# Regrouping the first columns of an input projection, and pinning the first solve on VectorE, in a FoX and RWKV-7 layer

## The chip, the cores and the metric

The kernel runs on one core of a Trainium2 chip. The metric is the device time of one execution in microseconds (us), and the time before is the median of three runs. PE is TensorE, the matrix engine; DVE is VectorE; ACT is ScalarE; POOL is GpSimd; SP is SyncE, which here does nothing but issue DMA transfers. Each engine works through its own list of instructions in the order in which they were placed at compile time and waits where an operand or a buffer is not ready.

## The reference

One layer over 256 tokens of width 4096, in float32. One input projection feeds two groups of heads and a gate; the two are joined, gated, projected, and added to the residual with a LayerNorm:

```
proj = einsum('bsd,dc->bsc', x, w_in)      # q,k,v,f | r,k,v,w_down,a_down | z
fox  = attention(q, k, v, cumsum(log_sigmoid(f + f_bias)))          # 16 heads of 128
r,k,v,w,a = token_shift(rw columns, mu_shift)
decay = exp(-exp(-softplus(-(w0 + tanh(w) @ w_up)) - 0.5));  a = sigmoid(a0 + a @ a_up)
y = rwkv7_scan(r, decay, k, v, -kk, kk * a)                         # 32 heads of 64
h = concat(fox, groupnorm(y) + bonus) * silu(z)
x = layernorm(ALPHA * x + h @ w_out)
```

The low-rank parts `w_down` and `a_down` have 96 columns each, and the forget gate `f` has 16: together the 208 columns that the kernel calls LoRA columns.

## The kernel before, in words

**The projections.** A float32 operand is split into a rounded high part and the remainder (`split`, L136 to L142): ACT casts the high part (L140), DVE subtracts (L141). A product of two such operands takes three matmuls (`mm`, L144 to L148): high by high (L146), low by high (L147), high by low (L148). The stationary operand is a 128 by 128 piece of the transposed tokens, the moving one a row of weights, up to 512 columns wide. The contraction runs over 32 slices of 128 (`KT`).

**The opening (L109 to L171).** It computes the 208 LoRA columns and the first block of 512 projection columns together, since the tokens are loaded and split at the same time. The slices come in 17 pieces, two of one slice and fifteen of two. Each piece brings tokens (`xr`), LoRA weights (`lr`) and main weights (`wr`). For each piece PE does the LoRA matmuls (into `accl`, two PSUM tiles for the two halves of the tokens) and then the 512-column ones (into `acc0_0`).

**The pairs.** After that the work goes by 8 pairs `n` of RWKV heads (each pair also with two FoX heads), each with four blocks `b` of 512 columns, each of 16 weight chunks of two slices; `w_3_7` is chunk 7 of block 3 of the current pair, and the profile leaves the numbers of pair and block out and writes `w_7`. A chunk is 12 matmuls. Chunks are prefetched: raw weights in 4 buffers (`wr`), high parts in 4, low parts in 3. While PE multiplies, generators are advanced by one step every six matmuls (`slot()`): they turn `bk` (the block's result, copied from PSUM) through DRAM, prepare the chunk matrices, run FoX attention and the RWKV recurrence.

**The solve (`rwkv`, L573 to L586).** For each pair the inverse of triangular 32 by 32 blocks is formed by 31 back-substitution steps on DVE. Each step is a product (L579, into `prod`) and a sum (L582, into `xc`), and each is one step of the generator. The result goes to DRAM (`td`) and back (`T`), is transposed into `X` (L610), and PE uses `T` and `X` in `qt` (L616) and `xp` (L637).

**What sets the order.** The compiler's list scheduler orders each engine's instructions by priorities and modelled times. `tc.keep_in_program_order(...)` pins one instruction to its place in the program among those of its engine. In the solve only the first product of each pair (`if not t`) is pinned. DMA transfers issued by SP form one queue in a fixed order: one that waits holds all behind it.

**The forget gate.** `lora()` transposes the LoRA result on PE (`lwt` L309, `fft` L312), and `forget()` turns it into a cumulative sum that goes to DRAM as `ncd` (L351), by way of `flg` (L350). `lw`, the copy of the LoRA result, shares one buffer with `bk` (tag `bk`), so the first `bk` is filled only when the transposes have read `lw`.

Of the kernel before, what the change touches and what calls it, by code (L numbers as in the profile page):

```python
# [10 lines left out]
F32 = mybir.dt.float32  # L11
# [6 lines left out]
P = 128  # L18
S = 256
D = 4096  # L20
KT = D // P
# [12 lines left out]
OB = 512  # L34
# [24 lines left out]
C_ROW = C_SCAN + S  # L59
C_W = C_ROW + 2  # L60
LW = 2 * LORA + NF


def constants():
# [17 lines left out]


@with_exitstack
def layer(ctx: ExitStack, tc: tile.TileContext, xt, xtok, w_lora, w_main, muv, w_o, up, par, mulora, fbias, lng, lnb, cst, out):
    nc = tc.nc
    PS = bass.MemoryType.PSUM

# [24 lines left out]
    for n, (k0, k1) in enumerate(pieces):  # L113
        raw = spool.tile([P, 2 * S], F32, tag="xr", name=f"xr{n}", bufs=4)
        nc.sync.dma_start(out=raw[:, : (k1 - k0) * S], in_=xt[:, k0:k1, :].rearrange("p k t -> p (k t)"))
        x_raw.append(raw)
        raw = spool.tile([P, 2 * LW], F32, tag="lr", name=f"lr{n}", bufs=4)
        (nc.scalar if n < 3 else nc.sync).dma_start(out=raw[:, : (k1 - k0) * LW], in_=w_lora[:, k0:k1, :].rearrange("p k c -> p (k c)"))
        l_raw.append(raw)
        raw = wpool.tile([P, 1024], F32, tag="wr", name=f"wr{n}", bufs=4)  # L120
        nc.sync.dma_start(out=raw[:, : (k1 - k0) * OB], in_=w_main[0, 0][:, k0:k1, :].rearrange("p k c -> p (k c)"))
        w_raw.append(raw)
    warm = const.tile([1, 1], F32, name="warm")
    nc.vector.memset(warm, 0.0)
# [12 lines left out]
    def split(src, n, name, pool=wpool, tag="", cols=1024):  # L137
        hi = pool.tile([P, cols], F32R, tag="wh" + tag, name=name + "h", bufs=4 if pool is wpool else 1)
        lo = pool.tile([P, cols], F32R, tag="wl" + tag, name=name + "l")
        nc.scalar.copy(hi[:, :n], src[:, :n])  # L140
        nc.vector.tensor_tensor(lo[:, :n], src[:, :n], hi[:, :n].bitcast(F32), ALU.subtract)  # L141
        return hi, lo  # L142

    def mm(acc, at, k, hi, lo, o, n):  # L144
        tt = slice(at * P, (at + 1) * P)
        nc.tensor.matmul(acc[:, :n], xs[k][:, 0, tt], hi[:, o : o + n], start=(k == 0), stop=False)  # L146
        nc.tensor.matmul(acc[:, :n], xs[k][:, 1, tt], hi[:, o : o + n], start=False, stop=False)  # L147
        nc.tensor.matmul(acc[:, :n], xs[k][:, 0, tt], lo[:, o : o + n], start=False, stop=(k == KT - 1))  # L148
# [8 lines left out]
    for n, (k0, k1) in enumerate(pieces):  # L157
        for k in range(k0, k1):
            t = xpool.tile([P, 2, S], F32R, tag=f"x{k}", name=f"x{k}")
            r = x_raw[n][:, (k - k0) * S : (k - k0 + 1) * S]  # L160
            tc.keep_in_program_order(nc.scalar.copy(t[:, 0, :], r))
            nc.vector.tensor_tensor(t[:, 1, :], r, t[:, 0, :].bitcast(F32), ALU.subtract)
            xs.append(t)
        hi, lo = split(l_raw[n], (k1 - k0) * LW, f"wl{n}", spool, str(n % 3), 2 * LW)
        for j, m in steps(k1 - k0, False):
            mm(acc_l[m], m, k0 + j, hi, lo, j * LW, LW)
        hi, lo = split(w_raw[n], (k1 - k0) * OB, f"wr{n}")
        for j, m in steps(k1 - k0, k1 == KT):
            mm(acc_0[m], m, k0 + j, hi, lo, j * OB, OB)
    early.close()  # L170

    half = const.tile([P, 2, G], F32, name="half")
# [123 lines left out]
        return r  # L296

    lr = const.tile([LORA, 2, 2, S], F32R, name="lr")
    lw = rp.tile([P, 2, LW], F32, tag="bk", name="lw")
    for m in range(2):  # L300
        nc.scalar.copy(lw[:, m, :], acc_l[m][:, :LW])
    ff = []

    def lora():
# [200 lines left out]
    def rwkv(n):  # L505
# [71 lines left out]
        for t, s in enumerate(range(B - 2, -1, -1)):  # L577
            w = B - 1 - s
            first = nc.vector.tensor_tensor(prod[:, :, :, s + 1 :], nb[:, :, s : s + 1, s + 1 :].to_broadcast([P, 2, NJ, w]), xc[:, :, :, s + 1 :], ALU.mult)  # L579
            if not t:  # L580
                tc.keep_in_program_order(first)
            nc.vector.tensor_reduce(xc[:, :, :, s : s + 1], prod[:, :, :, s:], AX.X, ALU.add)  # L582
            next(other, None)
            if t % ROWS == ROWS - 1:
                yield
# [453 lines left out]
def arrange(inputs):  # L1039
# [9 lines left out]
    res["w_lora"] = np.ascontiguousarray(np.concatenate([wd, ad, ff], 1).reshape(KT, P, LW).transpose(1, 0, 2))  # L1049
# [35 lines left out]
```

## Time and profile before

| | |
|---|---|
| median of three runs | 1958.2 us (1957.36 to 1959.06) |
| profiled execution, span from first to last instruction | 1956.1 us |
| PE busy | 1937.4 us, 99% |
| DVE busy | 1368.3 us, 70% |
| ACT busy | 981.2 us, 50% |
| mean DMA rate | 215 GB/s |
| granted TensorE clock, mean | 0.998 |

The profile gives the span of the one profiled execution and no other time for it; the median of the runs is 2.1 us above that span, and this difference is kept as it is. PE is busy for almost the whole span, so time can be won only where PE waits, or where its matmuls take more time than their columns need. In the timelines a row has start, duration, engine, line, operation, output and inputs, form and count, and in square brackets the idle time before it with what ended it. Matmuls overlap: their pace is read from the distance between starts, not from their durations.

### The profile page before, as it was taken

The page shows a single profiled execution, that of the slowest core. Times are in us where ns is not written, and L with a number is a line of the kernel's source. Part 1 is how long each engine was busy: PE and PEld are TensorE (multiplying, and loading weights), DVE is VectorE, ACT ScalarE, POOL GpSimd, SP SyncE. Part 2 cuts the span into 40 slices and gives each one's busy share as a digit, 9 for nine tenths or more (in the row PEclk, how much of TensorE's full clock was granted, in tenths as well). Part 3 has the DMA queues.
Part 4 walks back from the last instruction along what each step waited for, and adds up shares of the span by engine and source line. Part 5 has one row for each costly group of instructions (what it writes and reads, how often), then busy time and mean ns, then how long its engine had stood idle before and what let it go on. Part 6 is the DMA issues. An engine that isn't in the chain of part 4 may idle for free.

```text
span 1956.1 us, 28202 instructions
## 1 busy us (share of the span) xinstructions
PE 1937.4 (99%) x10169; PEld 1586.9 (81%) x10169; DVE 1368.3 (70%) x2212; ACT 981.2 (50%) x1485; POOL 81.2 (4%) x111
## 2 busy tenths in 40 slices
PE   9998999999999999999999999999999999999998
PEld 7887778888887888788878887888788878888886
DVE  6587667866886688667857785778577856755555
ACT  6553555455545554565456545644564454433332
POOL 0010001000100010001000100010001000000000
PEclk9999999999999999999999999999999999999999
DMA  9577657867686778676867686778677777766564
GB/s 337 145 237 198 206 163 244 226 194 213 212 233 186 215 215 232 192 220 208 232 185 225 208 236 183 225 209 234 178 231 211 241 274 236 255 199 199 189 198 168
DMA packets 269392, 420.13 MB, mean 215 GB/s; under 512 B 142338, under 2 KB 171028, under 8 KB 269252
## 3 DMA queue, kind: packets, MB, share of 16 engines
q1 hardware_dynamic: 268820, 417.91, 70.7%
q8 instruction: 80, 1.31, 0.3%
q10 hardware_dynamic: 432, 0.43, 0.1%
q14 instruction: 60, 0.49, 0.1%
HBM read 388.61 MB, written 29.64 MB: 214 GB/s over the span
## 4 chain that ended last, share of the span: by engine, by line
PE 86%; DMA 1%; DVE 0%; ACT 0%; issue 0%; DVEq 0%; ACTq 0%; SPq 0%
PE acc L146 21%; PE acc L148 20%; PE acc L147 20%; PE oacc L852 6%; PE oacc L854 6%; PE oacc L853 6%; PE yp L678 1%; PE gp L517 1%; PE up L653 1%; PE rh L626 1%; PE sp L662 0%; DMA wo<-in_w_o_dram 0%; PE fsp L717 0%; PE fop L736 0%; PE tp L550 0%; DMA h<-hd 0%
## 5 line engine op out<-in xcount | busy, mean ns | idle before, releaser
L582 DVE TENSOR_REDUCE xc<-prod 128x8 f32<-128x16 f32 (+30 forms) x248 | 73.2, 295 | 6.7
L579 DVE TENSOR_TENSOR prod<-Nb,xc 128x8 f32<-128x8 f32 (+30 forms) x248 | 71.6, 289 | 6.6
L141 DVE TENSOR_TENSOR w_10l<-w,w_10h 128x1024 fp32r<-128x1024 f32 x31 | 37.9, 1223 | 37.8 <-PE acc L148 21.6
L141 DVE TENSOR_TENSOR w_6l<-w,w_6h 128x1024 fp32r<-128x1024 f32 x31 | 38.9, 1256 | 34.9 <-ACT w_6h L140 18.6
L141 DVE TENSOR_TENSOR w_8l<-w,w_8h 128x1024 fp32r<-128x1024 f32 x31 | 37.8, 1219 | 32.9 <-ACT UV L656 13.6
L141 DVE TENSOR_TENSOR w_0l<-w,w_0h 128x1024 fp32r<-128x1024 f32 x31 | 37.9, 1222 | 31.3 <-ACT w_0h L140 14.8
L141 DVE TENSOR_TENSOR w_5l<-w,w_5h 128x1024 fp32r<-128x1024 f32 x31 | 38.3, 1235 | 29.3 <-PE acc L148 17.4
L148 PE MATMUL acc<-w_7l,x 128*128 128x512 f32 x124 | 49.5, 399 | 5.4 <-DVE w_7l L141 5.4
L141 DVE TENSOR_TENSOR w_7l<-w,w_7h 128x1024 fp32r<-128x1024 f32 x31 | 37.9, 1222 | 22.3 <-PE acc L148 13.2
L141 DVE TENSOR_TENSOR w_11l<-w,w_11h 128x1024 fp32r<-128x1024 f32 x31 | 37.9, 1222 | 21.0 <-PE acc L148 13.5
L141 DVE TENSOR_TENSOR w_12l<-w,w_12h 128x1024 fp32r<-128x1024 f32 x31 | 37.5, 1211 | 20.6 <-PE acc L148 16.1
L141 DVE TENSOR_TENSOR w_14l<-w,w_14h 128x1024 fp32r<-128x1024 f32 x31 | 38.0, 1227 | 19.9 <-issue 11.1
L140 ACT CAST w_0h<-w 128x1024 fp32r<-128x1024 f32 x31 | 32.7, 1053 | 38.3 <-PE acc L147 21.7
L140 ACT CAST w_5h<-w 128x1024 fp32r<-128x1024 f32 x31 | 32.6, 1053 | 37.9 <-PE acc L147 37.9
L140 ACT CAST w_8h<-w 128x1024 fp32r<-128x1024 f32 x31 | 32.6, 1050 | 37.7 <-DMA w<-in_w_main_dram 31.3
L146 PE MATMUL acc<-w_7h,x 128*128 128x512 f32 x124 | 51.0, 411 | 0.0
L140 ACT CAST w_13h<-w 128x1024 fp32r<-128x1024 f32 x31 | 32.5, 1049 | 36.4 <-PE acc L147 22.9
L146 PE MATMUL acc<-w_5h,x 128*128 128x512 f32 x124 | 50.5, 408 | 0.0
L146 PE MATMUL acc<-w_8h,x 128*128 128x512 f32 x124 | 50.0, 404 | 0.4 <-ACT w_8h L140 0.4
L140 ACT CAST w_9h<-w 128x1024 fp32r<-128x1024 f32 x31 | 32.4, 1046 | 35.6 <-PE acc L147 32.9
L146 PE MATMUL acc<-w_3h,x 128*128 128x512 f32 x124 | 50.2, 405 | 0.0
L140 ACT CAST w_7h<-w 128x1024 fp32r<-128x1024 f32 x31 | 32.6, 1052 | 34.9 <-PE acc L147 19.7
(813 smaller groups left out, 6549.3 us busy)
## 6 DMA issues: line engine op xcount, KB each, us to landing
w<-in_w_main_dram SPq DMA_DIRECT2D x496, 512.0 KB, 3.9
wo<-in_w_o_dram SPq DMA_DIRECT2D x128, 512.0 KB, 3.8
bt<-bk SPq DMA_DIRECT2D x88, 128.0 KB, 4.0
Nb<-nd SPq DMA_DIRECT2D x16, 512.0 KB, 5.0
wr<-in_w_main_dram SPq DMA_DIRECT2D x15, 512.0 KB, 7.1
hd<-hl SPq DMA_DIRECT2D x29, 256.0 KB, 4.4
h<-hd SPq DMA_DIRECT2D x29, 256.0 KB, 6.1
raw<-bt SPq DMA_DIRECT2D x16, 256.0 KB
```

What stands on the lines that cost most here:

```text
L140: nc.scalar.copy(hi[:, :n], src[:, :n])
L141: nc.vector.tensor_tensor(lo[:, :n], src[:, :n], hi[:, :n].bitcast(F32), ALU.subtract)
L146: nc.tensor.matmul(acc[:, :n], xs[k][:, 0, tt], hi[:, o : o + n], start=(k == 0), stop=False)
L147: nc.tensor.matmul(acc[:, :n], xs[k][:, 1, tt], hi[:, o : o + n], start=False, stop=False)
L148: nc.tensor.matmul(acc[:, :n], xs[k][:, 0, tt], lo[:, o : o + n], start=False, stop=(k == KT - 1))
L517: nc.tensor.matmul(gp[u][j][:, c * P : (c + 1) * P], BK[h, u, c, :], lt[j][h, u, c, :], start=True, stop=True)
L579: first = nc.vector.tensor_tensor(prod[:, :, :, s + 1 :], nb[:, :, s : s + 1, s + 1 :].to_broadcast([P, 2, NJ, w]), xc[:, :, :, s + 1 :], ...
L582: nc.vector.tensor_reduce(xc[:, :, :, s : s + 1], prod[:, :, :, s:], AX.X, ALU.add)
L626: nc.tensor.matmul(rh[HALF[j], u * C : (u + 1) * C], lt[j][:, u, c, 0:C], SV[j][:, u, c, :], start=True, stop=True)
L852: nc.tensor.matmul(acc, ht[k][:, 0, tt], hi, start=(k == 0), stop=False)
L853: nc.tensor.matmul(acc, ht[k][:, 1, tt], hi, start=False, stop=False)
L854: nc.tensor.matmul(acc, ht[k][:, 0, tt], lo, start=False, stop=(k == KT - 1))
```

## The change

Two things change. First, in the opening the LoRA array gets 128 more columns: it holds the 208 LoRA columns and the first 128 of the first block (`LA` = 336), and the rest of the first block comes from an array of its own with 384 columns (`LB`). Both are laid out on the host. The sum of the columns stays 720, and the first block's result is put together from both accumulators: `bk_0` takes its first 128 columns from `accl` and the rest from `acc0_0`. `lw` moves from tag `bk` to tag `vs`, so that it and `bk_0` no longer share a buffer. Second, in the first pair's solve (`n` = 0) all 31 products are pinned in program order on DVE, where before only the first was.

```diff
@@ constants
+LA = LW + P
+LB = OB - P
@@ layer: loads of the opening
-        raw = spool.tile([P, 2 * LW], F32, tag="lr", name=f"lr{n}", bufs=4)
+        raw = spool.tile([P, 2 * LA], F32, tag="lr", name=f"lr{n}", bufs=4)
...
-        nc.sync.dma_start(out=raw[:, : (k1 - k0) * OB], in_=w_main[0, 0][:, k0:k1, :].rearrange("p k c -> p (k c)"))
+        nc.sync.dma_start(out=raw[:, : (k1 - k0) * LB], in_=w_first[:, k0:k1, :].rearrange("p k c -> p (k c)"))
@@ matmuls of the opening
-        hi, lo = split(l_raw[n], (k1 - k0) * LW, f"wl{n}", spool, str(n % 3), 2 * LW)
+        hi, lo = split(l_raw[n], (k1 - k0) * LA, f"wl{n}", spool, str(n % 3), 2 * LA)
         for j, m in steps(k1 - k0, False):
-            mm(acc_l[m], m, k0 + j, hi, lo, j * LW, LW)
-        hi, lo = split(w_raw[n], (k1 - k0) * OB, f"wr{n}")
+            mm(acc_l[m], m, k0 + j, hi, lo, j * LA, LA)
+        hi, lo = split(w_raw[n], (k1 - k0) * LB, f"wr{n}")
         for j, m in steps(k1 - k0, k1 == KT):
-            mm(acc_0[m], m, k0 + j, hi, lo, j * OB, OB)
+            mm(acc_0[m], m, k0 + j, hi, lo, j * LB, LB)
@@ results of the opening
-    lw = rp.tile([P, 2, LW], F32, tag="bk", name="lw")
+    lw = rp.tile([P, 2, LW], F32, tag="vs", name="lw", bufs=1)
+    bk_0 = rp.tile([P, 2, OB], F32, tag="bk", name="bk0_0")
     for m in range(2):
         nc.scalar.copy(lw[:, m, :], acc_l[m][:, :LW])
+        nc.scalar.copy(bk_0[:, m, :P], acc_l[m][:, LW:LA])
@@ rwkv: the solve
-            if not t:
+            if not t or not n:
                 tc.keep_in_program_order(first)
@@ the pairs: the block's result
-            bk = rp.tile([P, 2, OB], F32, tag="bk", name=f"bk{n}_{b}")
+            bk = rp.tile([P, 2, OB], F32, tag="bk", name=f"bk{n}_{b}") if n or b else bk_0
...
+                elif not n and not b:
+                    nc.scalar.copy(bk[:, m, P:], acc[m][:, :LB])
@@ arrange (host)
+    first = res["w_main"][0, 0]
+    lora = np.concatenate([wd, ad, ff], 1).reshape(KT, P, LW).transpose(1, 0, 2)
+    res["w_lora"] = np.ascontiguousarray(np.concatenate([lora, first[:, :, :P]], 2))
+    res["w_first"] = np.ascontiguousarray(first[:, :, P:])
```

The order of instructions differs in the first pair up to the end of its solve; from there on every engine's list reads as before. Three places matter below. The line numbers of the changed kernel are 2 to 9 higher.

The first is DVE in the last third of the first pair's solve. `w_3_6l` to `w_3_8l` are the subtractions for chunks 6 to 8 of block 3; `prod` and `xc` are the solve's products and sums, and the last number of a product is its width. Before, the list ends the solve like this:

```order
L579 TENSOR_TENSOR prod_1691<-Nb_1547,xc_1692 128x8x28
L582 TENSOR_REDUCE xc_1692<-prod_1691 128x8
L579 TENSOR_TENSOR prod_1691<-Nb_1547,xc_1692 128x8x29
L582 TENSOR_REDUCE xc_1692<-prod_1691 128x8
L579 TENSOR_TENSOR prod_1691<-Nb_1547,xc_1692 128x8x30
L582 TENSOR_REDUCE xc_1692<-prod_1691 128x8
L579 TENSOR_TENSOR prod_1691<-Nb_1547,xc_1692 128x8x31
L582 TENSOR_REDUCE xc_1692<-prod_1691 128x8
L141 TENSOR_TENSOR w_3_7l<-w_3_7_1804,w_3_7h 128x1024
```

Between `w_3_6l` and `w_3_7l` stand 27 solve instructions, from the sum of step 18 to that of step 31. In the changed kernel DVE has between the same two:

```order
L143 TENSOR_TENSOR w_3_6l<-w_3_6_1776,w_3_6h 128x1024
L583 TENSOR_TENSOR prod_1693<-Nb_1549,xc_1694 128x8x12
L586 TENSOR_REDUCE xc_1694<-prod_1693 128x8
L583 TENSOR_TENSOR prod_1693<-Nb_1549,xc_1694 128x8x13
L586 TENSOR_REDUCE xc_1694<-prod_1693 128x8
L143 TENSOR_TENSOR w_3_7l<-w_3_7_1806,w_3_7h 128x1024
L583 TENSOR_TENSOR prod_1693<-Nb_1549,xc_1694 128x8x14
L586 TENSOR_REDUCE xc_1694<-prod_1693 128x8
L583 TENSOR_TENSOR prod_1693<-Nb_1549,xc_1694 128x8x15
L586 TENSOR_REDUCE xc_1694<-prod_1693 128x8
```

The steps are now two to a chunk, and the solve ends later in the list, just ahead of the subtraction for chunk 1 of the next pair's first block (`w_0_1l`).

The second place is SP's queue some chunks after the opening, while PE is in block 1 of the first pair. `bt` and `raw` are the turned result of block 0 on its way to DRAM and back, `ncd` is the forget gate's sum. Before:

```order
L218 DMA w_1_6_982<-in_w_main_dram 128x1024
L893 DMA muv_862<-in_muv_dram 128x256
L218 DMA w_1_7_1017<-in_w_main_dram 128x1024
L281 DMA bt_0_1002<-bk_0_859 64x16x32 x3
L351 DMA ncd<-flg 16x256
L281 DMA bt_0_1002<-bk_0_859 64x16x32
L218 DMA w_1_8_1037<-in_w_main_dram 128x1024
L218 DMA w_1_9_1055<-in_w_main_dram 128x1024
```

In the changed kernel the same queue reads:

```order
L220 DMA w_1_6_984<-in_w_main_dram 128x1024
L417 DMA upt_939<-in_up_dram 96x256
L899 DMA muv_864<-in_muv_dram 128x256
L283 DMA bt_0_1004<-bk_0_844 64x16x32 x4
L355 DMA ncd<-flg 16x256
L220 DMA w_1_7_1019<-in_w_main_dram 128x1024
L283 DMA raw_1037<-bt_0_1004 128x2x256
L220 DMA w_1_8_1039<-in_w_main_dram 128x1024
```

The load of chunk 7 now stands behind `ncd`, where before chunk 8 was the first load behind it.

The third place is PE at the start of block 1 of the first pair, 9 matmuls after the first of the block (`w_1_0h`). Before:

```order
L146 MATMUL acc_1_0_864<-w_1_1h,x_247 128x512
L147 MATMUL acc_1_0_864<-w_1_1h,x_247 128x512
L148 MATMUL acc_1_0_864<-w_1_1l,x_247 128x512
L309 MATMUL lwt<-cs,lw 96x128 x4
L312 MATMUL fft<-cs,lw 16x128 x2
L146 MATMUL acc_1_0_864<-w_1_1h,x_250 128x512
```

and in the changed kernel, where 18 matmuls of the block stand ahead of them:

```order
L148 MATMUL acc_1_1_867<-w_1_1h,x_247 128x512
L149 MATMUL acc_1_1_867<-w_1_1h,x_247 128x512
L150 MATMUL acc_1_1_867<-w_1_1l,x_247 128x512
L313 MATMUL lwt<-cs,lw 96x128 x4
L316 MATMUL fft<-cs,lw 16x128 x2
L148 MATMUL acc_1_0_866<-w_1_1h,x_250 128x512
```

The transposes of the LoRA result moved back by nine matmuls.

More of the change, by code (lines that the diff above doesn't have):

```diff
@@ L84, in layer @@
 @with_exitstack
-def layer(ctx: ExitStack, tc: tile.TileContext, xt, xtok, w_lora, w_main, muv, w_o, up, par, mulora, fbias, lng, lnb, cst, out):
+def layer(ctx: ExitStack, tc: tile.TileContext, xt, xtok, w_main, w_lora, w_first, muv, w_o, up, par, mulora, fbias, lng, lnb, cst, out):
     nc = tc.nc
@@ L116, in layer @@
         x_raw.append(raw)
-        raw = spool.tile([P, 2 * LW], F32, tag="lr", name=f"lr{n}", bufs=4)
-        (nc.scalar if n < 3 else nc.sync).dma_start(out=raw[:, : (k1 - k0) * LW], in_=w_lora[:, k0:k1, :].rearrange("p k c -> p (k c)"))
+        raw = spool.tile([P, 2 * LA], F32, tag="lr", name=f"lr{n}", bufs=4)
+        (nc.scalar if n < 3 else nc.sync).dma_start(out=raw[:, : (k1 - k0) * LA], in_=w_lora[:, k0:k1, :].rearrange("p k c -> p (k c)"))
         l_raw.append(raw)
         raw = wpool.tile([P, 1024], F32, tag="wr", name=f"wr{n}", bufs=4)
-        nc.sync.dma_start(out=raw[:, : (k1 - k0) * OB], in_=w_main[0, 0][:, k0:k1, :].rearrange("p k c -> p (k c)"))
+        nc.sync.dma_start(out=raw[:, : (k1 - k0) * LB], in_=w_first[:, k0:k1, :].rearrange("p k c -> p (k c)"))
         w_raw.append(raw)
@@ L1048, in arrange @@
     res["xtok"] = np.ascontiguousarray(x)
-    res["w_lora"] = np.ascontiguousarray(np.concatenate([wd, ad, ff], 1).reshape(KT, P, LW).transpose(1, 0, 2))
     types = (r, k, v, fv, fq, fk, zf, zr)
```

## The prediction

> **What bounds the kernel now.** I read the page first, then the list of PE's waits, then the busy times of three stretches, and last the timelines of the places that these point to.
>
> ```profile
> span 1956.1 us, 28202 instructions
> PE 1937.4 (99%) x10169; PEld 1586.9 (81%) x10169; DVE 1368.3 (70%) x2212; ACT 981.2 (50%) x1485; POOL 81.2 (4%) x111
> ...
> PE acc L148 <- DVE w_7l L141: 5.4, 1, 5.4
> ...
> PE acc L148 <- DVE w_8l L141: 1.0, 1, 1.0
> PE acc L146 <- ACT w_8h L140: 0.4, 1, 0.4
> ...
> 4.24:9.64 5.40, 5.40 (x24) 3.86 (x25) 3.62 (x9) 3.46 (x8) 0.00 (x0) 1.00 0.98 342
> 9.64:71.13 61.49, 61.49 (x361) 53.88 (x360) 38.49 (x67) 34.13 (x64) 2.47 (x3) 1.00 0.79 278
> ...
> 186.30:203.85 17.55, 11.14 (x41) 8.24 (x40) 12.24 (x27) 5.30 (x11) 0.00 (x0) 0.90 0.28 85
> ```
>
> PE bounds the kernel: 1937 of 1956 us. Of its waits one is large, 5.4 us for a DVE subtraction of chunk 7. The three stretches (length, then busy time of PE, weight loads, DVE, ACT and POOL, then granted clock, DMA share and GB/s) show the opening, in which PE never pauses after its first two pieces, and one place, 186.3 to 203.9, in which PE is busy for only 11.1 of 17.6 us and the granted clock falls to 0.90. Both parts of the change touch just these stretches.
>
> **Part one: the pinned solve.** PE's timeline around the wait, and DVE's just ahead of it:
>
> ```profile
> 183.57 0.39 PE L146 MATMUL acc<-w_6h,x 128*128 128x512 f32 x1
> 186.29 0.39 PE L146 MATMUL acc<-w_7h,x 128*128 128x512 f32 x1
> 192.27 0.79 PE L148 MATMUL acc<-w_7l,x 128*128 128x512 f32 x1 [5.37 <-DVE w_7l L141]
> 192.87 0.63 PE L146 MATMUL acc<-w_7h,x 128*128 128x512 f32 x1
> 193.29 0.63 PE L147 MATMUL acc<-w_7h,x 128*128 128x512 f32 x1
> 198.96 0.73 PE L148 MATMUL acc<-w_8l,x 128*128 128x512 f32 x2 [1.04 <-DVE w_8l L141]
> 199.53 0.39 PE L146 MATMUL acc<-w_8h,x 128*128 128x512 f32 x1
> 199.76 0.39 PE L147 MATMUL acc<-w_8h,x 128*128 128x512 f32 x1
> 203.85 0.40 PE L146 MATMUL acc<-w_10h,x 128*128 128x512 f32 x1
> ...
> 179.15 1.22 DVE L141 TENSOR_TENSOR w_6l<-w,w_6h 128x1024 fp32r<-128x1024 f32 x1
> 180.29 0.31 DVE L582 TENSOR_REDUCE xc<-prod 128x8 f32<-128x152 f32 x1
> ...
> 190.67 0.42 DVE L582 TENSOR_REDUCE xc<-prod 128x8 f32<-128x256 f32 x1
> 191.01 1.21 DVE L141 TENSOR_TENSOR w_7l<-w,w_7h 128x1024 fp32r<-128x1024 f32 x1
> ```
>
> A chunk takes 2.72 us (183.57 to 186.29). On DVE 27 solve instructions in a row, 180.29 to 191.01, stand ahead of the subtraction for chunk 7, and PE waits. From the start of chunk 7 to that of chunk 10 pass 17.56 us. Three chunks are 8.16 us, and the two score matmuls of FoX attention that lie in the stretch add about 0.45 us, an estimate of two matmul steps at the pace above. So the burst costs 17.56 - 8.61 = 8.95 us: the wait of 5.4, the slow pace behind it (0.42 us from 192.87 to 193.29, where it is 0.23 at 199.53), and smaller waits for chunks 8 and 9, whose subtractions the burst made late too. The Trainium skill (TensorE: Matmul & The Clock Gate, the part on the HAM clock gate) says that the array drops to half its clock after an idle window of about 3.4 us and is back after as much work. The trace agrees: half the pace after 5.4 us, full pace after 1.0. By that rule a new wait costs no more than itself while it stays under 3.4 us.
>
> In the changed list the same work stands between `w_3_0l` and `w_0_1l`, two steps to a chunk, so no chunk waits for a burst. It remains to see whether DVE gets through it in time.
>
> ```profile
> 162.07:219.96 57.89, 45.67 (x106) 0.97 0.64 188
> ...
> 224.41 0.39 PE L148 MATMUL acc<-w_1l,x 128*128 128x512 f32 x1
> ```
>
> From its start of `w_0l` to that of `w_1l` DVE is busy for 45.67 of 57.89 us. PE used `w_1l` first at 224.41; without the 8.95 us this is 215.46, and the subtraction, 1.2 us long, must start at 214.2, which is 52.1 us after 162.07. So 6.4 us are left for waits of DVE itself, on buffers that PE still reads and on arriving weights. DVE will have about that much: it waits for low-part buffers whenever it is three chunks ahead, and the last six steps come with eight `SV` subtractions and no chunk between them, so that `w_0_1l` comes about 7 us behind `w_0_0l`, against the 2.72 us that PE needs for a chunk. I expect a remaining wait of PE of 1.2 us, near that place; the bounds are 0 and 3 us. Net gain 8.95 - 1.2 = 7.7 us, 6.0 to 8.9.
>
> What is late next is the solve's way through DRAM:
>
> ```profile
> 214.06 3.74 SPq L591 DMA_DIRECT2D T<-td  x8
> ...
> 233.56 0.62 PE L616 MATMUL qt<-T,gb 32*32 32x32 f32 x27
> ```
>
> Before, the loads of `T` were issued at 214.06 to 217.8 and `qt` ran at 233.56, a margin of some 16 us. In the changed list the solve ends at about 214.5 in the old clock; the store takes some 2.5 us, the eight issues 3.7, the landing perhaps 3 (estimates from the same queue), so `T` is there at 224, and PE reaches `qt` at 233.56 - 7.7 = 225.9. The margin falls to 2 us, but holds; this costs nothing.
>
> **Part two: 336 and 384 columns.** The pace of three widths, from starts in the opening and from six 256-column matmuls elsewhere:
>
> ```profile
> 58.91 0.26 PE L146 MATMUL accl<-wl14h,x 128*128 128x208 f32 x1
> 60.24 0.41 PE L146 MATMUL acc<-wr14h,x 128*128 128x512 f32 x1
> 62.99 0.26 PE L146 MATMUL accl<-wl15h,x 128*128 128x208 f32 x1
> ...
> 113.94 0.28 PE L426 MATMUL lp<-lr,uph 96*128 96x256 f32 x1
> ...
> 114.65 0.40 PE L146 MATMUL acc<-w_14h,x 128*128 128x512 f32 x1
> ```
>
> Twelve matmuls of 208 columns take 1.33 us, 0.111 each; twelve of 512 take 2.75 (2.72 in the steady state, 0.227 each); six of 256 take 0.71, 0.118 each. By columns, 208 should take 0.092: the narrow ones have a floor. A piece takes 62.99 - 58.91 = 4.08 us now. If 336 and 384 run at the rate of 512 (0.443 ns a column), a piece takes 12 x 720 x 0.443 ns = 3.83 us, a gain of 0.25. If they lie on the straight line between 256 and 512, they take 0.152 and 0.172, a piece 3.89, a gain of 0.19. Fifteen pieces gain 2.8 to 3.8 us; I take 3.3. The Trainium skill (the same page, on loading the stationary operand and on the back-to-back gap) gives 128 columns / 1.2 = 107 ns for a weight load and N / 2.4 + 2.5 ns for a matmul. That makes 107 + 216 before and 142.5 + 162.5 after, 17.8 ns less for each of 180 pairs, 3.2 us by that estimate, and the trace's 0.111 fits the 107.
>
> The gain counts only if nothing else becomes the bound. From 9.64 to 71.13 DVE was busy 38.5 of 61.5 us and ACT 34.1, with the same elements to split afterwards. The same bytes in 58 us need 278 x 61.5 / 58 = 295 GB/s, under the 342 of the first 5.4 us. The first two pieces took 2.70 us each for 2.04 us of matmuls: they wait for arriving data, and the larger first LoRA piece (336 for 208 columns) is weighed up by the smaller main piece. Zero, with 0.4 us either way. The four extra ACT copies replace parts of others and stand behind the last LoRA matmul, beside PE.
>
> **Part three: the queue around the forget gate.** This follows from the earlier `bk_0` and the later transposes.
>
> ```profile
> 71.13 0.39 PE L146 MATMUL acc<-w_0h,x 128*128 128x512 f32 x1
> 73.18 0.60 PE L309 MATMUL lwt<-cs,lw 128*96 128x128 f32 x4
> ...
> 89.10 0.34 SPq L351 DMA_DIRECT2D ncd<-flg  x1
> 90.35 1.20 SPq L218 DMA_DIRECT2D w<-in_w_main_dram  x2
> ...
> 95.11 1.05 ACT L140 CAST w_8h<-w 128x1024 fp32r<-128x1024 f32 x1 [4.50 <-DMA w<-in_w_main_dram]
> ...
> 92.96 0.39 PE L146 MATMUL acc<-w_7h,x 128*128 128x512 f32 x1
> 96.21 0.50 PE L146 MATMUL acc<-w_8h,x 128*128 128x512 f32 x1 [0.37 <-ACT w_8h L140]
> 99.43 0.39 PE L146 MATMUL acc<-w_9h,x 128*128 128x512 f32 x1
> ```
>
> Before, `ncd` holds the queue until 89.10, chunk 8 is issued at 90.35 and lands at 95.11, and chunks 7 and 8 take 99.43 - 92.96 = 6.47 us for 5.44: 1.03 us lost. Now chunk 7 stands behind `ncd`. Counted from the block's first matmul (71.13), the transposes move from 2.05 to 4.1 us. From them to `ncd` it was 15.9 us on DVE and ACT; ahead of `flg` on DVE stand three chunk subtractions less (1.1 us each) and two `bk` transposes less (0.6 each), 4.6 us, but some of that time DVE will wait for buffers instead; I take 12. So `ncd` goes at 16.1, chunk 7 at 16.5, lands after the 4.8 us of before at 21.3, and its high part is there at 22.4 and its low part at 23.6. PE wants them at 21.8 and 22.7 (PE's order now has the four high products ahead). The wait is about 0.9 us, against 1.03 lost before: a gain of 0.1 us, between a loss of 2 (chain as long as before) and a gain of 1.
>
> **The sum.** 7.7 + 3.3 + 0.1 = 11.1 us. The profiled span would fall from 1956.1 to 1945.0, and the median, 2.1 us above it, from 1958.2 to 1947.1. Within 0.2% (3.9 us) a measurement of this kernel can't tell from no change.
>
> **The rivals.** *The stall moves.* DVE may be so full in the pinned stretch that a new wait of over 3.4 us arises, say at `w_0_1l`, with the slow pace behind it: 4 + 1.5 us lost in place of 1.2, and 1951.4. For it speaks the ledger with only 6.4 us to spare; against it that the other seven pairs, which show no such wait in the list, run their solve with one or two chunks between the steps. *The regrouping gives nothing*, because the opening is held by arriving data at the faster pace, and the queue loses its 2 us: 1958.2 - 7.7 + 2 = 1952.5. For it speaks a DMA share of 0.79 in the opening; against it that PE has no wait on data there. *Slower than before:* `qt` waits for `T`. If the solve ended so late that `T` lands after PE wants it, all later work of the pair's chain shifts and PE stands. To lose all of the gain the wait must reach 11 us, so that the solve would end 13 us later than reckoned, at about 227; to be measurably slower, at 231. At 14 us of wait the time is 1961. DVE would have to stand idle for that long between steps, and no row shows what for.
>
> **How the numbers follow.** The forecast holds with 0.77, the moved stall 0.09, the lost regrouping 0.10, the slower case 0.04. The forecast's own bounds are 7.7 + 3.3 + 0.1 with 6.0 + 2.4 - 2.0 = 6.4 at the low end and 8.9 + 4.2 + 1.0 = 14.1 at the high end, 1951.8 to 1944.1. I widen it by half a microsecond below for the runs' spread and to 1952.5 above, which takes in the first two rivals' centres. Faster by over 0.2% (below 1954.3): 0.93; within it 0.03; slower 0.04.
>
> **What would show it.** In the changed profile PE's largest wait in the first pair should be under 2 us and the granted clock 1.00 there; a piece of the opening should take 3.83 to 3.89 us from start to start; the wait at chunk 7 of block 1 should be under 2 us and chunk 8 should have none; `qt` should not wait. Wrong would be a PE wait over 3.4 us at any chunk from `w_3_3` to `w_0_1`, a wait of the opening on `wr` or `lr`, or a later pair that differs.

## The result and the profile after

| | before | changed |
|---|---|---|
| median of the executions, four each | 1957.9 us (1957.36 to 1959.06) | 1950.4 us (1949.29 to 1950.99) |
| profiled execution, span | 1956.1 us | 1949.2 us |
| ratio | | 0.9957, 95% interval 0.9945 to 0.9970 |

The changed kernel is faster by 7.5 us, two thirds of the forecast's 11.1. The time lies inside the forecast's range of 1943.6 to 1952.5. The page of the changed kernel and its list of PE's waits:

```profile
span 1949.2 us, 28205 instructions
PE 1934.7 (99%) x10169; PEld 1593.5 (82%) x10169; DVE 1366.5 (70%) x2212; ACT 982.8 (50%) x1487; POOL 84.8 (4%) x111
...
PE acc L148 <- ACT w_8h L142: 1.1, 1, 1.1
PE acc L150 <- DVE w_8l L143: 1.0, 1, 1.0
PE accl L148 <- ACT wl0h L142: 0.9, 1, 0.9
PE acc L150 <- DVE w_1l L143: 0.8, 1, 0.8
...
PE acc L148 <- ACT w_7h L142: 0.6, 1, 0.6
```

The wait of 5.4 us at `w_7l` is gone. The five shown, of 0.6 to 1.1 us, stand at other places; the one at `w_8l` was there before with the same 1.0, the others are new or longer. This profiled execution, 1950.99 us, is the slowest of the changed kernel's four. The busy times of four stretches of the changed kernel (length, then PE, weight loads, DVE, ACT, POOL, then granted clock, DMA share, GB/s), in the order: the opening's first two pieces, the other fifteen, block 1 up to chunk 12, and chunks 7 to 9 of block 3:

```profile
4.92:10.98 6.06, 6.06 (x25) 6.06 (x26) 4.58 (x10) 4.57 (x11) 0.00 (x0) 1.00 1.03 392
10.98:69.98 59.00, 59.00 (x362) 59.00 (x362) 38.32 (x67) 34.59 (x64) 1.83 (x3) 1.00 0.81 277
69.98:108.53 38.55, 36.69 (x161) 28.30 (x161) 30.26 (x51) 25.02 (x39) 2.23 (x8) 1.00 0.66 195
186.39:197.09 10.70, 9.46 (x42) 7.20 (x41) 7.12 (x17) 5.19 (x10) 0.00 (x0) 1.00 0.45 143
```

Place by place, by PE's starts of the same matmuls: the third piece starts at 10.98 us where it was 9.64, so the first two pieces lost 1.34. The other fifteen take 59.00 for 61.49, a gain of 2.49. Block 1 takes 38.55 to its chunk 12, before it was this:

```profile
71.13:108.48 37.35, 36.54 (x162) 28.41 (x160) 28.93 (x50) 25.19 (x40) 1.01 (x6) 1.00 0.62 184
```

So block 1 lost 1.20, and at its chunk 12 the profiled execution stands where it stood before (108.53 and 108.48). The stretch from `w_3_7` to `w_3_10` takes 10.70 for 17.56, a gain of 6.86, and `w_0_1` gives 1.07 of it back. At `w_0_2` the changed kernel is 5.7 us ahead. The remaining 1.2 us of the profiled difference come later, where the lists of both kernels read the same: 0.3 in the next block, 0.4 at `xp` of the last pair (its wait was 1.1 and is 0.7) and 0.6 in the output projection, with 0.2 lost in between. No run shows that the change causes them. Two things need an explanation: why 2.1 us stay lost after the solve's burst is gone, and where the regrouping's gain went.

The first shows in VectorE's timeline of the changed kernel, and TensorE's beside it:

```profile
184.15 0.29 DVE L586 TENSOR_REDUCE xc<-prod 128x8 f32<-128x128 f32 x1
189.97 0.74 DVE L726 SCALAR_TENSOR_TENSOR lg<-fsp,ct,nb 128x128 f32<-128x128 f32 x2 [5.53 <-PE fsp L721]
190.62 1.21 DVE L143 TENSOR_TENSOR w_8l<-w,w_8h 128x1024 fp32r<-128x1024 f32 x1
...
189.33 0.60 PE L721 MATMUL fsp<-fk,fq 128*128 128x256 f32 x2
...
191.89 0.73 PE L150 MATMUL acc<-w_8l,x 128*128 128x512 f32 x2 [1.03 <-DVE w_8l L143]
```

DVE stands idle for 5.53 us. The next instruction of its list adds the forget bias to the first head's FoX scores (`lg`), which PE computes (`fsp`) only behind chunk 7. The subtraction for chunk 8 is queued behind it. DVE has time enough, as e4 and e6 show below; the addition to the scores stands at the wrong place in its list.

The second shows in SP's queue and ACT's timeline in block 1:

```profile
86.62 0.33 SPq L355 DMA_DIRECT2D ncd<-flg  x1
86.99 0.42 SPq L220 DMA_DIRECT2D w<-in_w_main_dram  x1
87.60 1.01 SPq L283 DMA_DIRECT2D raw<-bt  x1
88.71 1.36 SPq L220 DMA_DIRECT2D w<-in_w_main_dram  x3
...
90.72 1.05 ACT L142 CAST w_7h<-w 128x1024 fp32r<-128x1024 f32 x1 [2.69 <-DMA w<-in_w_main_dram]
95.19 1.04 ACT L142 CAST w_8h<-w 128x1024 fp32r<-128x1024 f32 x1 [1.96 <-DMA w<-in_w_main_dram]
```

SP waits for `flg`, stores `ncd` at 86.62, then issues chunk 7, then the read of `raw`, then chunk 8 at 88.71. ACT, which waits for chunk 8, can cast it 6.5 us later, at 95.19.

### The profile page after: what moved, and what is told of

Same layout as the page of the kernel before. It is cut to its first block, busy times and chain, and to the rows that moved or that the text cites. A ratio compares the mean times of both kernels' runs of the same rounds, so it can differ in the third digit from the quotient of the medians.

```text
span 1949.2 us, 28205 instructions
## 1 busy us (share of the span) xinstructions
PE 1934.7 (99%) x10169; PEld 1593.5 (82%) x10169; DVE 1366.5 (70%) x2212; ACT 982.8 (50%) x1487; POOL 84.8 (4%) x111
## 4 chain that ended last, share of the span: by engine, by line
PE 97%; DMA 1%; DVE 1%; issue 0%; ACT 0%; SPq 0%; DVEq 0%; ACTq 0%
PE acc L148 24%; PE acc L150 23%; PE acc L149 23%; PE oacc L856 6%; PE oacc L858 6%; PE oacc L857 6%; PE yp L682 1%; PE gp L521 1%; PE up L657 1%; PE rh L630 1%; PE accl L148 1%; PE accl L149 1%; PE accl L150 1%; PE sp L666 0%; DMA h<-hd 0%; DMA wo<-in_w_o_dram 0%
## 5 line engine op out<-in xcount | busy, mean ns | idle before, releaser
L143 DVE TENSOR_TENSOR w_10l<-w,w_10h 128x1024 fp32r<-128x1024 f32 x31 | 37.9, 1222 | 37.4 <-PE acc L150 24.5
L143 DVE TENSOR_TENSOR w_6l<-w,w_6h 128x1024 fp32r<-128x1024 f32 x31 | 37.9, 1223 | 36.6 <-ACT w_6h L142 21.4
L143 DVE TENSOR_TENSOR w_7l<-w,w_7h 128x1024 fp32r<-128x1024 f32 x31 | 37.9, 1223 | 27.6 <-PE acc L150 13.2
L143 DVE TENSOR_TENSOR w_5l<-w,w_5h 128x1024 fp32r<-128x1024 f32 x31 | 37.9, 1223 | 26.9 <-PE acc L150 16.5
L143 DVE TENSOR_TENSOR w_11l<-w,w_11h 128x1024 fp32r<-128x1024 f32 x31 | 37.9, 1222 | 20.5 <-PE acc L150 13.5
L143 DVE TENSOR_TENSOR w_12l<-w,w_12h 128x1024 fp32r<-128x1024 f32 x31 | 37.6, 1212 | 20.9 <-PE acc L150 16.1
L717 POOL TENSOR_SCALAR_AFFINE_SELECT nb<-nb 128x128 f32<-128x128 f32 x32 | 19.4, 608 | 751.0 <-DMA nb<-ncd 288.9
L143 DVE TENSOR_TENSOR w_14l<-w,w_14h 128x1024 fp32r<-128x1024 f32 x31 | 37.9, 1221 | 17.6 <-issue 13.0
L142 ACT CAST w_2h<-w 128x1024 fp32r<-128x1024 f32 x31 | 32.7, 1054 | 34.2 <-PE acc L149 34.2
```

## The experiments

Times are medians in us; the difference is taken to the kernel before as it ran beside it on the same chip, and runs are compared by these differences. The ratio is not the quotient of the two medians, and its interval is 3.5 to 5.5 us wide. The intervals of all runs but e2 and e11 overlap with that of the changed kernel. So the times alone don't settle a difference of 1 to 3 us between two runs; below, the same place read in the profiles has to agree with it.

| run | median | difference | ratio, 95% interval |
|---|---|---|---|
| changed kernel | 1950.4 | -7.5 | 0.9957 (0.9945 to 0.9970) |
| e1 pinned solve alone | 1952.3 | -6.0 | 0.9972 (0.9961 to 0.9983) |
| e2 regrouping alone | 1956.6 | -1.6 | 0.9992 (0.9983 to 1.0001) |
| e3 eight warm-up matmuls | 1949.3 | -8.9 | 0.9957 (0.9943 to 0.9971) |
| e4 scores pinned | 1951.8 | -6.4 | 0.9968 (0.9955 to 0.9980) |
| e5 store on POOL's queue | 1947.7 | -10.7 | 0.9945 (0.9933 to 0.9958) |
| e6 scores pinned, near | 1950.1 | -8.3 | 0.9959 (0.9945 to 0.9973) |
| e7 four warm-up matmuls | 1951.2 | -7.2 | 0.9962 (0.9949 to 0.9974) |
| e8 e3, e5 and e6 together | 1948.8 | -9.6 | 0.9952 (0.9939 to 0.9964) |
| e9 e3 and e5 | 1947.6 | -10.7 | 0.9945 (0.9933 to 0.9958) |
| e10 e9, scores earlier, unpinned | 1945.9 | -12.5 | 0.9936 (0.9922 to 0.9949) |
| e11 before, store on POOL's queue | 1957.1 | -0.8 | 0.9997 (0.9988 to 1.0006) |
| e12 e11 and the pinned solve | 1950.3 | -7.6 | 0.9962 (0.9949 to 0.9974) |

### Each part alone: e1 and e2

e1 is the kernel before with one line changed:

```diff
-            if not t:
+            if not t or not n:
                 tc.keep_in_program_order(first)
```

> The kernel before with the first part of the change alone: the first pair's solve steps in order. Forecast's theory: 7.7 us less, 1950.2. Theory from the trace after: the stall at chunk 7 goes, but some 2 us stay between chunks 7 and 10 (VectorE waits for the FoX scores ahead of the subtraction for chunk 8) and 1.1 at w_0_1, so 5.8 to 7 us less, 1951 to 1952.2, with the stretch from the first matmul of w_3_7 to that of w_3_10 at 10.7 us and no slow pace in it. The opening and block 1 should stand as before: 71.1 us at w_1_0, about 1 us lost at chunk 8.

Measured: 6.0 us less. The stretch of e1 from `w_3_7` to `w_3_10`:

```profile
186.31:196.99 10.68, 9.48 (x42) 7.21 (x41) 7.10 (x17) 5.18 (x10) 0.00 (x0) 1.00 0.48 158
```

10.68 us with the clock at 1.00, as in the changed kernel. `w_0_2` is reached 5.7 us earlier than before, and the opening and block 1 stand as before. The pinned solve is worth about 6.0 us and not 7.7, as the second of the two expectations had it.

e2 is the changed kernel with that line put back.

> The changed kernel with the solve's steps as before. Forecast's theory: 3.4 us less than before, 1954.5. Theory from the trace after: the regrouping gains 2.5 us from the third piece on, loses 1.3 in the first two and 1.2 at chunks 7 and 8 of block 1, so nothing: 1957 to 1958.2, with the stall at w_3_7 back at its 5.4 us.

Measured: 1.6 us less, between the two expectations; the interval reaches to no change. The parts add within the intervals: 6.0 + 1.6 = 7.6, and the whole is 7.5. Here the regrouping, with what it does to the queue, is worth half of the 3.4 that the forecast gave it. In e2's profiled execution chunks 7 and 8 of block 1 take 9.70 us for the 6.47 of before:

```profile
90.30:100.00 9.70, 7.86 (x24) 5.39 (x25) 7.28 (x13) 6.10 (x10) 0.11 (x1) 0.82 0.87 292
...
95.47 0.50 PE L148 MATMUL acc<-w_8h,x 128*128 128x512 f32 x1 [1.79 <-ACT w_8h L142]
95.80 0.40 PE L149 MATMUL acc<-w_8h,x 128*128 128x512 f32 x1
...
98.17 0.63 PE L149 MATMUL acc<-w_8h,x 128*128 128x512 f32 x1
98.60 0.63 PE L150 MATMUL acc<-w_8l,x 128*128 128x512 f32 x1
```

A wait of 1.79 us, and then 0.43 us from start to start where 0.23 is the pace. This profiled execution is the slowest of e2's, 1959.8 us; its row tells where the time can go, the median how much goes there. The stall that is back from `w_3_7` to `w_3_10` takes 18.74 us in it, for the 17.56 of before.

### The queue: e5, e11 and e12

```diff
-        nc.sync.dma_start(out=ncd, in_=lg)
+        nc.gpsimd.dma_start(out=ncd, in_=lg)
```

e5 is the changed kernel with this line, e11 the kernel before with it, e12 is e11 with the solve pinned.

> The changed kernel with the forget gate's store issued by POOL's queue, so that SP goes on to chunks 7 and 8 of block 1 without waiting for flg. If SP's wait is what costs block 1 its 1.2 us, PE's waits of 0.6 and 1.1 at w_1_7h and w_1_8h go, block 1 from the first matmul of w_1_0 to that of w_1_12 falls from 38.55 us to 36.3 to 37, and the time falls by 1.2 to 2.2 us to 1948.2 to 1949.2. If the chunks are late because of their own transfer, of ACT's order or of the stores of bt, the waits stay and the time with them, 1950.4.

> The kernel before with the forget gate's store on POOL's queue and nothing else. The forecast reckoned that the store costs the kernel before 1.03 us at chunk 8 of block 1. If so, chunks 7 and 8 take 5.44 us in place of 6.47 and the time falls by 0.7 to 1.3 us, to 1957. If the gain of 2.7 us that POOL's queue gave the changed kernel is one of the queue itself and not of the changed order, it falls by 2 to 3 us, to 1955.5.

> The kernel before with the pinned solve and the store on POOL's queue, that is the run e5_ncd_pool without the regrouping. With the queue out of the way the distance to e5's 1947.7 is the regrouping alone. The forecast's theory gives it 3.3 us, and this run 1951.0; the pace of the trace after, 0.15 us a piece for 15 pieces less 0.5 in the first two, gives 1.8 us, and this run 1949.5. The sum of the parts found so far, 6.0 for the solve and 1.0 for the queue, says 1951.2.

Measured: e5 takes 3.2 us off the changed kernel (10.7 less than before for 7.5), e11 0.8 off the kernel before (its interval includes no change; what moved is read from the trace), e12 stands at 7.6 below before. e5 gained more than the 1.2 to 2.2 that were expected; e12 lies between its expectations. In e11's profile PE is 1.15 us ahead at chunk 12 of block 1 and only 0.33 at `w_3_10`, since the unpinned stall takes 18.34 us for 17.56. Chunks 7 and 8 of block 1 in e12 and in e5, and ACT's casts for them in e5:

```profile
93.13:98.57 5.44, 5.44 (x26) 4.50 (x24) 5.14 (x10) 4.03 (x7) 0.10 (x1) 1.00 0.68 211
...
90.22:95.66 5.44, 5.44 (x25) 4.50 (x24) 5.39 (x12) 4.81 (x8) 0.11 (x1) 1.00 0.84 246
...
87.09 1.04 ACT L142 CAST w_7h<-w 128x1024 fp32r<-128x1024 f32 x1
88.04 1.04 ACT L142 CAST w_8h<-w 128x1024 fp32r<-128x1024 f32 x1
```

5.44 us is twice a chunk's 2.72, with nothing lost; so it is in all six runs with the store on POOL's queue (e5, e8, e9, e10, e11, e12). With the store on SP's queue the two chunks take 6.46 and 6.47 in the two profiles without the regrouping, and 6.5 to 9.7 in the six with it, not counting up to 1.3 us of waiting ahead of chunk 7. The loss at chunk 8 of the kernel before is 1.03, as the forecast reckoned.

The four corners, all with the solve pinned, give the regrouping's worth. With SP's queue: e1 to the changed kernel, 7.5 - 6.0 = 1.5 us. With POOL's queue: e12 to e5, 10.7 - 7.6 = 3.1 us. So by the medians the regrouping by itself gives about the forecast's 3.3, and 1.6 of it is lost in the queue. The intervals are too wide to show these two numbers by themselves; the rows agree with their direction. From its first matmul to chunk 12, block 1 takes 37.4 us in before and e1 and 36.0 in e11 and e12: the store on SP's queue costs 1.4. With the regrouping it takes 37.9 to 40.2 in the six profiles with SP's queue and 35.2 in the four with POOL's: there the store costs 2.7 to 5.0. In e5 the scheduler also put the read of `raw` behind chunk 8's load; whether the hold by `ncd` or the place of `raw` costs more isn't separated.

Of the 3.1, 2.9 are found along PE's list: `w_1_0` starts at 69.13 in e5 and at 71.25 in e12, 2.1 us earlier, and block 1 to its chunk 12 takes 35.18 for 35.97. The two profiled executions are only 1.9 us apart at their ends, so 1.0 of the lead is lost again later on. The rows of block 1, and PE's wait for DVE at `ctp` in e12, which e5 does not have:

```profile
71.25:107.22 35.97, 35.72 (x161) 28.66 (x160) 29.20 (x50) 25.24 (x41) 1.95 (x8) 1.00 0.74 212
...
87.97 0.29 PE L355 MATMUL ctp<-cs,frest 16*128 16x16 f32 x2 [0.23 <-DVE frest L349]
...
69.13:104.31 35.18, 35.18 (x161) 28.75 (x161) 30.43 (x51) 25.08 (x40) 2.59 (x9) 1.00 0.76 217
```

### The opening's first two pieces: e3 and e7

In the changed kernel's profile the opening's first matmul comes 0.87 us after the warm-up matmuls and runs at half pace, 0.28 us from start to start:

```profile
4.92 0.65 PE L148 MATMUL accl<-wl0h,x 128*128 128x336 f32 x1 [0.87 <-ACT wl0h L142]
5.36 0.48 PE L149 MATMUL accl<-wl0h,x 128*128 128x336 f32 x1
5.64 0.48 PE L148 MATMUL accl<-wl0h,x 128*128 128x336 f32 x1
...
9.46 0.32 PE L148 MATMUL accl<-wl1h,x 128*128 128x336 f32 x1
9.61 0.33 PE L149 MATMUL accl<-wl1h,x 128*128 128x336 f32 x1
```

e3 sets `WARM` to 8, e7 sets it to 4; it was 6.

> The changed kernel with eight warm-up matmuls in place of six, so that they last until about 4.9 us and leave no gap ahead of the first real matmul. If the half pace of 4.9 to 9.3 us comes from the 0.87 us gap after the warm-up, the first matmuls of 336 columns start 0.15 us apart from the outset, the third piece starts at 9.7 to 9.9 in place of 10.98, and the time falls by 1.1 to 1.3 us against the changed kernel, to about 1949.2. If arriving data is what holds PE in the first two pieces, waits for x, wl1 or wr1 take the place of the slow pace, the third piece starts at 10.8 to 11.0 and the time stays at 1950.4.

> The changed kernel with four warm-up matmuls in place of six, so that a gap of 1.5 us or more lies ahead of the first real matmul in every execution. If the gap decides the pace, the first two pieces run at half pace (336 columns 0.28 us apart) until 8 us or later, the third piece starts at 10.7 to 11.2, and the time is 0.5 to 1.5 us above the changed kernel, whose executions have the half pace only now and then, 1951 to 1952. If the half pace came from something else, the third piece starts at 8.8 to 9.8 and the time stays at 1950.4.

e3 is 8.9 us below before where the changed kernel is 7.5, with the third piece at 9.39 and the pace at 0.15 from the start:

```profile
4.91 0.32 PE L149 MATMUL accl<-wl0h,x 128*128 128x336 f32 x1
5.07 0.32 PE L148 MATMUL accl<-wl0h,x 128*128 128x336 f32 x1
```

e7 is 7.2 below, with a gap of 1.39 us, half pace until 9.2 and the third piece at 10.77. Both moved the way the gap's theory says, e7 by 0.3 us where 0.5 to 1.5 were expected, and both intervals overlap with that of the changed kernel. The times don't show it, and the ratio of e3, 0.9957, is that of the changed kernel; the pace of the matmuls shows it. Between e3 and e7 lies a spread that was not expected. The openings of the changed kernel, e2, e4, e5 and e6 are the same code, with gaps of 0.87, 0.56, 0.51, 0.32 and 0.34 us, and reach full pace at 9.4, 4.9, 4.8, 6.1 and 6.7 us. The four runs with eight warm-up matmuls all reach it by 5.5. And where the pace is full early, PE waits for the next piece's tokens instead, up to 1.15 us at `wl1h` in e9. So the third piece starts anywhere from 8.77 to 10.98 in the ten profiles with the regrouping, at 10.1 on average, and at 9.4 to 9.7 in the four without it. The 1.34 us of the changed kernel's profile are the worst of ten; 0.5 is the mean.

The longer warm-up does not bring the third piece forward: the mean is 10.08 us in the four profiles with eight matmuls and 10.03 in the five with six. What orders the profiles is when the second piece's tokens arrive. ACT starts to cast them at 5.59 us in e2, 6.25 in e3, 6.61 in e4, 6.83 in e5, 6.85 in e10 and 7.04 in e9, and the third piece starts 3.13 to 3.18 us after that in all six. In e6 and e8 ACT waits 0.81 us more for the second piece's main weights, and it is 3.6 and 3.7. Only in the changed kernel's profile and in e7, where the half pace lasts beyond 9 us, it is 4.3 and 4.0: there the slow pace costs about 1 us. So in eight of the ten profiles it is arriving data that holds the third piece, which was the rival in e3's expectation, and in two the half pace.

### The scores' place: e4 and e6

```diff
-            nc.vector.scalar_tensor_tensor(lg[:, blk, :], spv[:, blk, :], ...)
+            score = nc.vector.scalar_tensor_tensor(lg[:, blk, :], spv[:, blk, :], ...)
+            if not i:
+                tc.keep_in_program_order(score)
```

e6 has the same and `yield from wait(1 if not i else W["fs"])` ahead of the score matmuls, where `W["fs"]` is 4.

> The changed kernel with the first head's FoX score instruction on VectorE held in the program's order too, so that it stands behind the subtraction for chunk 12 and not ahead of that for chunk 8. If VectorE's 5.5 us wait for the scores is what makes chunk 8 late, that wait goes, PE's wait of 1.0 at w_3_8l goes, the stretch w_3_7 to w_3_10 falls from 10.7 to 8.6 or 8.7, and the wait at w_0_1l goes as well or shrinks, since the solve's steps move forward by some 5 us: 2 to 3 us less, 1947.4 to 1948.4. If VectorE has simply too much work in this stretch, the wait only moves to a later chunk and the time stays within 0.5 us of 1950.4.

> As the run with the scores held in order, but their start is moved three slots earlier, so that on VectorE they stand behind the subtraction for chunk 9 and one solve step, on TensorE half a chunk earlier, and the triangular products (qt) are no longer cut into four groups. If it was the scores' place that cost the time at chunk 8, and the splitting of qt and the pushed-back solve that ate the gain in the run before, the stretch w_3_7 to w_3_10 is 8.7 to 9.2 us, w_0_1l waits under 0.8, and the time falls by 1 to 2 us against the changed kernel, to 1948.4 to 1949.4. If VectorE is full there, a wait of 1 us or more turns up at w_0_1l or at qt and the time stays within 0.5 us of 1950.4.

Both do what was asked of them: from `w_3_7` to `w_3_10` they take 8.84 us for the changed kernel's 10.70, with PE never idle.

```profile
186.79:195.63 8.84, 8.84 (x41) 7.36 (x40) 8.14 (x22) 5.65 (x9) 0.00 (x0) 1.00 0.81 272
```

And yet neither is clearly faster. By the medians e4 lies 1.1 us behind the changed kernel, outside both of its expectations, and e6 0.8 ahead, with the wait at `qt` that its second one named. The 1.9 us are lost again around `qt`, which waits for `T` and is cut into groups. In e4 the wait at `w_0_1l` grows as well, from 0.75 to 1.47 us. e6 at `qt`, and its queue, in a profiled execution that is the slowest of its five, 1952.4 us:

```profile
226.53 0.44 PE L620 MATMUL qt<-T,gb 32*32 32x32 f32 x16
227.43 0.24 PE L620 MATMUL qt<-T,gb 32*32 32x32 f32 x2 [0.46 <-DMA T<-td]
230.11 0.43 PE L620 MATMUL qt<-T,gb 32*32 32x32 f32 x14 [1.32 <-DMA T<-td]
...
217.17 1.79 SPq L220 DMA_DIRECT2D w<-in_w_main_dram  x2
219.01 0.91 SPq L593 DMA_DIRECT2D td<-xc  x2
220.09 0.33 SPq L220 DMA_DIRECT2D w<-in_w_main_dram  x1
223.76 3.64 SPq L595 DMA_DIRECT2D T<-td  x8
```

With the scores held back, the solve's last step came at 218.5 us in e6 where it was 216.5 in the changed kernel, and its store `td` went out behind two weight loads. `T` was read 4.8 us after the store was issued; in the changed kernel it was 2.0 (216.95 and 218.97). This is the forecast's slower rival in small: its margin of 2 us for `T` was small indeed, and the first change that moved the pair 2 us forward used it up.

### Together: e8, e9 and e10

e8 is e3, e5 and e6 in one kernel; e9 is e3 and e5; e10 is e9 with a single further edit, and nothing more pinned:

```diff
-        yield from wait(W["fs"])
+        yield from wait(0 if not i else W["fs"])
```

> Eight warm-up matmuls, the store on POOL's queue and the scores near their place, together. If the three losses are what keeps the change from its 11 us, they add: 1.1 + 1.5 + 1.5 us less than the changed kernel, 1946.3, within 1945.3 to 1947.5. If VectorE or the queue gives the time back elsewhere, less than half of that, above 1948.3.

> The changed kernel with eight warm-up matmuls and the store on POOL's queue, the scores left where they are. The two repairs touch different stages, so they should add: e5's 1947.7 less the part of the half pace that e5's executions still had, 0.3 to 1.1 us: 1946.6 to 1947.4. If the time e8 lost came from these two and not from the scores' place, it stays near 1948.8.

> As the run beside it, and the first head's score matmuls are started four slots earlier, with nothing pinned: on TensorE half a chunk earlier, on VectorE still ahead of the subtraction for chunk 8; the solve ends ahead of w_0_1l as in the changed kernel, its store stands ahead of the loads of w_0_5 and w_0_6, and qt is in one piece. If the late T is what ate the gain in e6 and e8 (its store behind two weight loads, the solve's end behind w_0_1l), qt does not wait here, the stretch w_3_7 to w_3_10 falls from 10.7 to 9.2 to 9.9 us and the time lies 0.8 to 1.5 us under the run beside it. If whatever moves the pair forward makes qt wait, qt waits 1 us or more here too and the two runs are equal within 0.5 us.

e8, at 1948.8, is no faster than e5, of which it has everything, and above the 1948.3 of its second expectation. In its profile, the slowest of its five executions, the lead over the kernel before is 11.3 us at the next pair's first matmul and 6.9 one block later, where e5 goes from 11.0 to 10.2. `qt` waits 1.7 us for `T`, and the matmuls behind it run at half pace for 3 us. The stretch behind the second of these waits, with its granted clock of 0.59, and two of its rows:

```profile
226.56:230.50 3.94, 3.94 (x23) 3.17 (x24) 2.52 (x4) 1.41 (x2) 0.00 (x0) 0.59 0.93 312
...
226.56 0.43 PE L620 MATMUL qt<-T,gb 32*32 32x32 f32 x14 [1.16 <-DMA T<-td]
...
228.08 0.63 PE L149 MATMUL acc<-w_5h,x 128*128 128x512 f32 x1
```

e9 is as fast as e5, just above the 1946.6 to 1947.4 that were expected. Its pace is full from the start, but PE waits for the second piece's tokens (1.15 us at `wl1h`), and its third piece starts at 10.17 where e5's does at 9.97. So e3's gain can't be relied on. e10 is the fastest, 1945.9, 1.7 us under e9, where 0.8 to 1.5 were expected (the ranges, 1945.5 to 1947.1 and 1946.6 to 1949.7, overlap a little) and 12.5 under the kernel before. Its stretch from `w_3_7` to `w_3_10`, its queue at the end of the solve, and `qt`, which doesn't wait:

```profile
182.30:192.22 9.92, 9.50 (x44) 7.56 (x43) 7.47 (x19) 4.91 (x11) 0.00 (x0) 1.00 0.50 159
...
212.49 0.80 SPq L593 DMA_DIRECT2D td<-xc  x2
213.62 0.33 SPq L220 DMA_DIRECT2D w<-in_w_main_dram  x1
214.09 3.81 SPq L595 DMA_DIRECT2D T<-td  x8
...
222.97 0.69 PE L620 MATMUL qt<-T,gb 32*32 32x32 f32 x32
```

Here the score matmuls come half a chunk earlier on PE, so that DVE waits 4.72 us for them and not 5.53, and the first transposes of the attention weights now fall into the same stretch. The solve's end stays ahead of `w_0_1l` and its store ahead of the loads.

## Why the prediction was right, and where it fell short

**The pinned solve: 7.7 forecast, 6.0 measured (e1), at the lower bound.** The mechanism held: no chunk waits for the burst, the largest wait around the solve is 1.0 us, and the clock stays at 1.00. The rest near `w_0_1l` was forecast at 1.2 and measured at 1.07. The step that failed is the ledger of VectorE, which found 6.4 us to spare and spent them on waits for buffers and arriving weights. A wait for the FoX scores, 5.5 us in the changed kernel, stood in the same stretch. It was to be read in the timeline of before, just behind the rows that were used:

```profile
197.03 0.74 DVE L722 SCALAR_TENSOR_TENSOR lg<-fsp,ct,nb 128x128 f32<-128x128 f32 x2 [4.81 <-PE fsp L717]
```

There it cost the 1.04 us at `w_8l`, which the forecast put down to the burst. It outlived the burst, with 2.1 us lost between `w_3_7` and `w_3_10` (10.70 for the forecast's 8.61). Of these, 1.86 are the scores' place: without it the stretch takes 8.84 in e4 and e6, with PE never idle. The other 0.23 are the forecast's own: it counted two score matmuls there, and the rows show four.

**The regrouping: 3.3 forecast, 3.1 measured with the queue out of the way (e12 to e5).** The sum came out near by luck, with terms that were not right. A piece takes 59.00 / 15 = 3.93 us, not 3.83 to 3.89: 336 columns take 0.152 us, as the straight line said, and 384 take 0.1755 where it said 0.172. That is 2.5 us and not 3.3 in the changed kernel's profile. The first two pieces, forecast at zero with 0.4 either way, swing from 0.9 better to 1.3 worse with the arrival of the second piece's tokens, 0.5 worse on average; that arriving data holds them was forecast, its spread was not. And block 1 to its chunk 12 became 0.8 us shorter (35.97 to 35.18), which the forecast didn't count; PE's wait at `ctp` is part of that, the rest is open.

**The queue: a gain of 0.1 forecast, a loss of 1.6 by the medians, within the bounds of 2 lost and 1 gained.** The times of the chain were good: `ncd` at 16.6 us after the block's start for 16.1 forecast, chunk 7's wait 0.6 for 0.9. What failed is the statement that chunk 8 should have no wait. It has one of 1.07. The read of `raw` now stands between the loads of chunks 7 and 8 and put off the issue of chunk 8 from 87.4 at the earliest to 88.71, and chunk 8 could be cast 6.5 us after its issue, for the 4.8 that the forecast took for a landing. How much is due to the read and how much to the hold by `ncd` stays open.

**The rule on the slow pace** (TensorE: Matmul & The Clock Gate in the Trainium skill, the HAM clock gate) was used to say that a wait under 3.4 us costs no more than itself. It held for the 1.03 us at `w_8l`, and not in e2, where a wait of 1.79 us was followed by 3 us at half pace, nor in e8, where waits of 0.51 and 1.16 us within 3 us were.

**The rivals.** The stall did not move as one large wait. The regrouping's lost gain with the queue's loss was named as a rival at 1952.5; what happened is most of its second half, 1.6 of 2 us, with the regrouping's gain still there. `qt` did not wait for `T` in the changed kernel, but did as soon as the pair moved forward.

The sum as measured by the medians is 6.0 + 3.1 - 1.6 = 7.5 us. A time near the forecast's 11.1 was to be had: e5, with the store alone moved, is at 10.7, and e10, with two edits more, at 12.5.

## What to carry to other kernels

Before counting an engine's idle time as slack, read in its timeline what it waits for: a wait for another engine did not shrink here when work was spread out around it (4.81 us before, 5.53 after), and the fix is then the waiting instruction's place, not less work. When a change moves one store earlier in an in-order queue, follow the two or three transfers behind it to their landing, since a store that waits for an operand charges its wait to all of them; another queue costs one line. And after each gain look at the chain with the smallest margin, as here `T` with its 2 us, because the next gain can be lost there.

## What the runs showed of the hardware

**Half pace starts after less idle time than expected, and not always.** After 5.4 us idle the matmuls of before ran at half pace, after 1.03 and 1.07 in the changed kernel they did not, after 1.79 in e2 they did: 0.43 us apart, from 96.3 to 99.5. The row of that stretch shows a granted clock of 0.82. In e8 they did from 227.7 to 230.6, behind waits of 0.51 and 1.16 us, with a granted clock of 0.59. After 1.36 in e9 and 1.47 in e4 they did not, nor in e6 after 0.46 and 1.32, which add up to as much as in e2. What decides it is not shown.

**The pace of the first matmuls differs from run to run.** With one and the same code, 336-column matmuls ran 0.28 us apart until 4.8, 4.9, 6.1, 6.7 or 9.4 us, with gaps behind the warm-up of 0.51, 0.56, 0.32, 0.34 and 0.87 us: the longer gap doesn't go with the longer half pace. With eight warm-up matmuls and no gap full pace was there by 5.5 in four of four profiles. The Trainium skill (the same page and section) says that the activity window runs freely, so that the point of change varies from run to run, by 0.5 us either way in its measurement; here it varies as well, but over 4.6 us. The granted clock of the profile's row for 4.92 to 10.98 reads 1.00 although almost three quarters of it ran at half pace; there only the distance between starts tells.

**A small store behind large loads lands late.** `td` (two stores of 64 KB) was ready for its readers 2.0 us after its issue ahead of the weight loads, and 4.8 us behind two of them (e6, and the same in e8). No run moves the loads alone, so that they are the cause is argued and not shown.
